# Weight chunks of the attention stage split by casting and accumulating DMAs from one pool of nine slots

## The chip, the core and the metric

The kernel runs on one core of one Trainium2 chip. The time is the device time of one execution in microseconds (us); the figure for a kernel is the median of its runs. Names used throughout: PE is TensorE, DVE is VectorE, ACT is ScalarE, POOL is GpSimd, SP is SyncE, whose queue issues most of the loads.

## What is computed

One layer of a streaming encoder on 256 tokens of width 2048, in float32. The cut below leaves out the shapes.

```python
h = rmsnorm(x, norm_in)
z, xbc, dt, q, k, v, gate_a, q_idx, k_idx, w_idx, gates = split(h @ w_in)
y_m = ssd_branch(z, xbc, dt, ...)       # causal convolution, chunked scan, silu gate, group norm
y_a = dsa_branch(q, k, v, gate_a, ...)  # index scores, top-64 keys of a query, softmax attention
g = sigmoid(gates + gate_bias)
merged = g[:, :D] * (y_m @ w_branch[:2048]) + g[:, D:] * (y_a @ w_branch[2048:])
x = rmsnorm(x + merged @ w_out, norm_final)
```

All the dense products stream their weights: `w_in`, `w_branch` and `w_out` lie in memory as 192 chunks `W[i]` of 128 x 2048 float32 (1 MiB each), in the order of use.

## The kernel before

**Split products.** A float32 product is made of three products of a shorter type (`F32R`): a weight chunk `raw` is rounded to `hi` by ACT (L121), and DVE forms the rest, `lo = raw - hi` (L122). The activations are kept as such a pair too (`xh`, `xl`). For every block PE adds `hi`·`xh`, `hi`·`xl` and `lo`·`xh` into one accumulator; so two of three products need `hi` alone, and every third one needs `lo`. With `hi` as stationary operand the result comes out transposed (`gemm_t`, `chunk_t`, L143 to L171: units "T" of two chunks, 48 products of 256 columns in each); with the activations stationary it comes out natural (`gemm_n`, `chunk_n`, L173 to L194: units "N" of four chunks, in each 12 products of 512 columns for either token block, accumulators `acc_n0` and `acc_n1`).

**The stream of weights.** `fetch` (L124) takes a `raw`, a `hi` and a `lo` tile, each from a pool of its own with three slots (L83 to L85), issues the load on SP (L134) and the split. `next_chunk` (L138) calls it until 1 + `AHEAD` = 3 chunks are ready, and hands out the oldest. `w_tiles` (L115) also serves the opening (L217 to L238), where x and the first two units' weights arrive in step in five pieces, and the small `w0` array (L246 to L249). `state["done"]` counts chunks consumed, `tick` (L105) then emits work that `after` (L101) put off.

**What sets the order.** The code is written as one program; a scheduler at build time lays the instructions out in one queue for each engine, by dependences and by when a slot of a pool comes free, and the engines run their queues in order. So where a chunk's split stands among the other work of ACT and DVE follows from the order in which the tiles of the pools are taken.

**The stages, in order**: the opening and the norm; four groups of the SSD mixer (`conv_silu`, `decay`, `natural_x`, `mix`, `transposed_y`, L373 to L470: DVE adds the skip term to PE's `py` at L435, makes the decays `E` at L393 and L396, ACT clips them at L399; the gate `sz` is evacuated at L479); the indexer and the top-k selection (`select`, L538: rounds of MAX8 and MATCH_REPLACE8, L550 and L551); branch A's gates and product; the `v` stage (four natural units, evacuated by ACT at L593); attention (eight rounds of three transposed units for keys, queries and gate, 48 chunks, with `attend`, `flip` and `weigh` of the heads between them); branch B's gates, and the second projection (four natural units: DVE multiplies by the gate, L690, adds to `merged`, L691, transposes it by 16 instructions, L680, ACT copies to `xh`, L682); the output product with the last norm.

Of the kernel before, what the change touches and what calls it, by code (L numbers as in the profile page):

```python
# [11 lines left out]
F32 = mybir.dt.float32  # L12
F32R = mybir.dt.float32r
# [17 lines left out]

# columns of the small-parameter array
PN, PCW, PCB, PGN, PDT, PAL = 0, 16, 112, 136, 152, 153
NPAR = 154
NWARM = 10  # products that bring the array to its full clock
PIECES = ((0, 2), (2, 4), (4, 8), (8, 12), (12, 16))  # row blocks of the first pieces
AHEAD = 2  # chunks of weights fetched ahead of the products


def unit_list():  # L40
    """The dense products in the order in which their weights stream in.

    ("T", source, first row, columns of the two blocks): transposed result, weights stationary.
    ("N", source, first row, first column): natural result, 512 columns, activations stationary.
    """
    us = []
    for g in range(4):
        us.append(("T", "in", 0, (B0 + 128 * g, C0 + 128 * g)))
        for a in range(2):
            c = XS0 + 512 * g + 256 * a  # L50
            us.append(("T", "in", 0, (c, c + 128)))
        us.append(("N", "in", 0, Z0 + 512 * g))
    for j in range(4):
        us.append(("T", "in", 0, (QI0 + 256 * j, QI0 + 256 * j + 128)))
    for j in range(4):
        us.append(("N", "in", 0, GM0 + 512 * j))
        us.append(("N", "br", 0, 512 * j))
    for j in range(4):
        us.append(("N", "in", 0, V0 + 512 * j))
    for j in range(8):  # L60
        for c in (K0, Q0, G0):
            us.append(("T", "in", 0, (c + 256 * j, c + 256 * j + 128)))
    for j in range(4):
        us.append(("N", "in", 0, GA0 + 512 * j))
    for j in range(4):
        us.append(("N", "br", D, 512 * j))
    for j in range(4):
        us.append(("N", "out", 0, 512 * j))
    return us


UNITS = unit_list()
NCHUNK = sum(2 if u[0] == "T" else 4 for u in UNITS)


@with_exitstack
def block_kernel(ctx, tc, W, w0, xT, xn, par, gbias, dsk, nf, out):
# [4 lines left out]
    acts = ctx.enter_context(tc.tile_pool(name="acts", bufs=1))  # L82
    wraw = ctx.enter_context(tc.tile_pool(name="wraw", bufs=3))  # L83
    whi = ctx.enter_context(tc.tile_pool(name="whi", bufs=3))
    wlo = ctx.enter_context(tc.tile_pool(name="wlo", bufs=3))  # L85
    dram = ctx.enter_context(tc.tile_pool(name="dram", bufs=1, space=DRAM))
# [8 lines left out]

    # ---------------------------------------------------------------- weights
    state = {"unit": 0, "chunk": 0, "done": 0}
# [3 lines left out]
    def after(n, fn):  # L101
        """Emit fn behind the products of the next n chunks, so that its operands are there in time."""
        pending.append((state["done"] + n, fn))
# [11 lines left out]
    def w_tiles():  # L115
        return (wraw.tile([P, 2048], F32, tag="raw", name="raw"),
                whi.tile([P, 2048], F32R, tag="hi", name="hi"),
                wlo.tile([P, 2048], F32R, tag="lo", name="lo"))

# [4 lines left out]
    def fetch(hi=None, lo=None):  # L124
        """Load the next chunk of weights and split it into two float32r parts."""
        i = state["chunk"]
        if i == NCHUNK:
            return
        state["chunk"] += 1
        if hi is None:  # L130
            raw, hi, lo = w_tiles()
        else:
            raw = wraw.tile([P, 2048], F32, tag="raw", name="raw")
        nc.sync.dma_start(raw, W[i])  # L134
        split(hi, lo, raw)
        ready.append((hi, lo))
# [24 lines left out]
    def gemm_t(ah, al):  # L161
        """acc[c, cb, t] = sum_k w[k, c] a[k, t] for the next transposed unit."""
        assert UNITS[state["unit"]][0] == "T"
        state["unit"] += 1
        acc = acc_tile("acc_t")
        for half in range(2):
            hi, lo = next_chunk()
            chunk_t(acc, hi, lo, half, range(8), ah, al)
            if half == 0:
                tick()  # L170
        return acc  # L171
# [11 lines left out]
    def gemm_n(ah, al):  # L183
        """acc[tb][t, c] for the next natural unit of 512 columns."""
        assert UNITS[state["unit"]][0] == "N"
# [9 lines left out]

    # ------------------------------------------------------- input, RMS norm
    part = const.tile([P, NPAR], F32, name="part")
# [14 lines left out]
    xTv = xT.rearrange("p (k t) -> p k t", t=T)  # L212
    # the array's clock rises under load: keep it busy until the first operands are there
    pw = aux_tile([P, P], "pw")
    for _ in range(NWARM):
        mm(pw, ones, ones, start=True, stop=True)
    # the first two units: x and their weights arrive in step, piece by piece  # L217
    acc_start = [acc_tile(f"acc_start{u}") for u in range(2)]
# [21 lines left out]
    for k0, k1 in PIECES:  # L240
# [3 lines left out]
                                axis=mybir.AxisListType.X, op=ALU.add)  # L244
    # k_idx (64), dt (32), w_idx (16)
    raw, hi, lo = w_tiles()  # L246
# [4 lines left out]
    for tb in range(2):  # L251
        for i, (k0, k1) in enumerate(PIECES):
            mm(prn[:, tb:tb + 1], xraw[:, k0, tb * P:tb * P + P], ones[:, 0:1],
               start=i == 0, stop=i == len(PIECES) - 1)
    # 1 / rms of every token: per partition, and along the free axis
    rn = const.tile([P, 2], F32, name="rn")
# [32 lines left out]

    # ------------------------------------------------ masks, dt and its sums  # L290
    tri = const.tile([P, 384], F32, name="tri")
# [31 lines left out]
    nc.vector.tensor_scalar(ab[H], dt[H], an[H], -1.0, ALU.mult, ALU.mult)  # L323
    # running sums within chunks of 64
    nc.vector.tensor_tensor_scan(al[H], rmask[H], ab[H], 0.0, ALU.mult, ALU.add)
# [37 lines left out]

    # -------------------------------------------------------------- SSD mixer

# [15 lines left out]
    def decay(g, acb, bc):  # L381
        """M[s, h, t] = exp(sum of dt a over s+1..t) (B_s . C_t) for t >= s, 0 before."""
        pcb = aux_tile([P, 384], "pcb")
# [34 lines left out]
    def mix(M, xdt, xD, sz):  # L418
        """Gated and normalised output of a group, natural layout."""
        ss = grp2.tile([P, 2], F32, tag="ss", name="ss")  # L420
# [66 lines left out]

    # ---------------------------------------------------------------- indexer
    mb = const.tile([P, 384], F32, name="mb")
# [3 lines left out]

    # keys for two heads at once: rows 0..63 give columns 0..255, rows 64..127 columns 256..511
    kbh = grp.tile([P, 2, T], F32R, tag="xdt", name="kbh")
# [8 lines left out]
    def index_scores(pair, qh, ql):  # L504
        """Adds the scores of heads 2 pair, 2 pair + 1 to sc."""
        cb = pair % 2
# [31 lines left out]
    def select():  # L538
        """mb: 0 for the keys that are chosen and finite, -BIG for the others."""
        # query chunk c sees the keys below 64 (c + 1)  # L540
        hidden = (slice(64, P), slice(P + 192, 384))
# [16 lines left out]

    # ------------------------------------------- branch A: gates and product
    def gates(acc, c0, out_ap):  # L560
        """sigmoid(projection + bias) of 512 columns, natural layout."""
        gb = tmp.tile([P, 512], F32, tag="gb", name="gb")
# [24 lines left out]

    # -------------------------------------------------------------- attention
    v = big.tile([P, 2, D], F32, tag="big", name="v")
# [7 lines left out]
    def attend(kT, qT, hh, le):  # L597
        """Attention weights of one head, natural layout, in blocks
        (queries 0, keys 0), (queries 1, keys 0), (queries 1, keys 1)."""
        pl = aux_tile([P, 384], "pl")  # L600
# [14 lines left out]
    def flip(les):  # L615
        """Keys on partitions: the same three blocks of both heads, each transposed."""
        t = tmp.tile([P, 2, 3, P], F32, tag="pT", name="pT", bufs=1)
# [42 lines left out]

    # ------------------------------------------- branch B: gates and product
    for j in range(4):
# [31 lines left out]

    # ---------------------------------------- output product, residual, norm
    x1 = big.tile([P, 2, D], F32, tag="big", name="x1")
# [11 lines left out]
    for j in range(4):  # L708
# [3 lines left out]
        if j < 3:  # L712
            if j == 2:
                # the last unit's four chunks stay on chip together
                hh = acts.tile([P, 2, 2048], F32R, tag="ya", name="hh")
                ll = acts.tile([P, 2, 2048], F32R, tag="yb", name="ll")
# [10 lines left out]
    for tb in range(2):  # L727
        r = rf[:, tb:tb + 1]
        # sum over the columns that are done, / D + EPS
        nc.vector.tensor_reduce(r, sf[:, tb, 0:3], axis=mybir.AxisListType.X, op=ALU.add)  # L730
# [73 lines left out]
```

## Time and profile before

| what | us |
|---|---|
| median of 3 runs | 1161.73 |
| lowest and highest run | 1160.87, 1162.21 |
| profiled execution: its span (the profile gives no other time of it) | 1159.6 |
| PE busy, of the span | 1146.9 (99%) |
| DVE busy | 753.6 (65%) |
| ACT busy | 544.1 (47%) |
| POOL busy | 13.4 (1%) |

The span runs from the first to the last instruction of one profiled execution. The rows of the section further down come from that execution: busy times of an engine in a stretch, mean durations of groups of instructions, and idle times with what ended them.

### The profile page before, as it was taken

The numbers are of one execution on the slowest core, as the hardware profiler recorded it, in microseconds if no ns is written. First come the engines' busy times: TensorE is split into PE (matmuls) and PEld (weight loads), VectorE is DVE, ScalarE is ACT, GpSimd is POOL, SyncE is SP. The second block draws the span as 40 slices with busy tenths as digits, with TensorE's granted clock in tenths as the row PEclk, the third lists the DMA queues.
The fourth block names the chain that finished last, engine by engine and source line by source line (L and its number), as shares of the span: only waits on it lengthen the run. The fifth ranks groups of instructions, "written<-read, shape, count | busy, mean of one in ns | idle before, by whom it ended". The sixth has DMA issues, their size and how long they took to land.

```text
span 1159.6 us, 16788 instructions
## 1 busy us (share of the span) xinstructions
PE 1146.9 (99%) x7174; PEld 1040.3 (90%) x7174; DVE 753.6 (65%) x931; ACT 544.1 (47%) x507; POOL 13.4 (1%) x29
## 2 busy tenths in 40 slices
PE   8999999999999999999999999999999999999997
PEld 8989898999988888888899999999999888888887
DVE  7899767685668445444447667766677455789662
ACT  7556765574444333334335434544444443343451
POOL 0001000000000000000000000000000000000000
PEclk9999999999999999999999999999999999999999
DMA  7755636354446556555554544545544566564652
GB/s 253 257 219 182 218 125 239 127 198 149 146 171 218 192 188 217 194 189 208 184 185 154 207 159 169 181 146 185 180 169 143 210 215 235 181 234 158 239 197 73
DMA packets 33979, 217.15 MB, mean 187 GB/s; under 512 B 3857, under 2 KB 4081, under 8 KB 9201
## 3 DMA queue, kind: packets, MB, share of 16 engines
q1 hardware_dynamic: 31248, 207.58, 51.0%
q10 hardware_dynamic: 2656, 8.50, 2.0%
q8 instruction: 56, 0.92, 0.3%
q14 instruction: 19, 0.15, 0.0%
HBM read 213.87 MB, written 2.13 MB: 186 GB/s over the span
## 4 chain that ended last, share of the span: by engine, by line
PE 93%; DVE 3%; DMA 2%; ACT 1%; issue 0%; POOLq 0%; DVEq 0%; SPq 0%; POOL 0%; ACTq 0%
PE acc_t L149 37%; PE acc_n L181 16%; PE acc_n L179 16%; PE acc_n L180 16%; DMA xraw<-xT 1%; DVE lo L122 1%; PE acc_last L181 1%; PE acc_last L180 1%; PE acc_last L179 1%; PE py L431 1%; PE py L433 1%; PE pl L602 1%; PE py L428 1%; PE po L629 1%; DMA raw<-W 1%; DVE c L376 1%
## 5 line engine op out<-in xcount | busy, mean ns | idle before, releaser
L122 DVE TENSOR_TENSOR lo<-raw,hi 128x2048 fp32r<-128x2048 f32 (+2 forms) x197 | 437.2, 2223 | 273.5 <-ACT hi L121 273.0
L121 ACT ACTIVATE hi<-raw 128x2048 fp32r<-128x2048 f32 (+2 forms) x197 | 366.3, 1861 | 468.2 <-PE acc_n L180 249.8
L149 PE MATMUL acc_t<-xh,hi 128*128 128x256 f32 x1216 | 320.9, 285 | 0.0
L149 PE MATMUL acc_t<-xl,hi 128*128 128x256 f32 x1216 | 317.9, 283 | 0.0
L149 PE MATMUL acc_t<-xh,lo 128*128 128x256 f32 x1216 | 244.9, 283 | 0.0
L181 PE MATMUL acc_n<-lo,xh 128*128 128x512 f32 x608 | 236.7, 389 | 0.3 <-DVE lo L122 0.3
L179 PE MATMUL acc_n<-hi,xh 128*128 128x512 f32 x608 | 237.0, 390 | 0.0
L180 PE MATMUL acc_n<-hi,xl 128*128 128x512 f32 x608 | 236.6, 389 | 0.0
L149 PEld LDWEIGHTS acc_t<-xl,hi 128*128 128x128 f32 x1216 | 233.4, 192 | 0.5
L149 PEld LDWEIGHTS acc_t<-xh,hi 128*128 128x128 f32 x1216 | 233.2, 192 | 0.5
L149 PEld LDWEIGHTS acc_t<-xh,lo 128*128 128x128 f32 x1216 | 189.6, 192 | 0.0
L181 PEld LDWEIGHTS acc_n<-lo,xh 128*128 128x128 f32 x608 | 114.1, 188 | 24.6 <-DVE lo L122 0.7
L180 PEld LDWEIGHTS acc_n<-hi,xl 128*128 128x128 f32 x608 | 114.2, 188 | 23.6
L179 PEld LDWEIGHTS acc_n<-hi,xh 128*128 128x128 f32 x608 | 114.2, 188 | 23.2
L180 PE MATMUL acc_n<-hi,yl 128*128 128x512 f32 x256 | 99.6, 389 | 0.0
L179 PE MATMUL acc_n<-hi,yh 128*128 128x512 f32 x256 | 99.6, 389 | 0.0
L181 PE MATMUL acc_n<-lo,yh 128*128 128x512 f32 x256 | 99.6, 389 | 0.0
L181 PEld LDWEIGHTS acc_n<-lo,yh 128*128 128x128 f32 x256 | 48.0, 188 | 10.3
L180 PEld LDWEIGHTS acc_n<-hi,yl 128*128 128x128 f32 x256 | 48.0, 188 | 10.0
L179 PEld LDWEIGHTS acc_n<-hi,yh 128*128 128x128 f32 x256 | 48.0, 188 | 9.8
L622 DVE STREAM_TRANSPOSE pT<-le 32x192 f32<-32x192 f32 x128 | 47.3, 370 | 1.9
L376 DVE SCALAR_TENSOR_TENSOR c<-u,part,c 128x255 f32<-128x255 f32 (+2 forms) x72 | 30.8, 479 | 2.0 <-ACT c L373 1.4
(201 smaller groups left out, 832.0 us busy)
## 6 DMA issues: line engine op xcount, KB each, us to landing
raw<-W SPq DMA_DIRECT2D x188, 1024.0 KB, 4.9
acb<-adr ACTq DMA_DIRECT2D x4, 1024.0 KB, 4.6
raw<-W SPq DMA_DIRECT2D x6, 512.0 KB, 8.6
gb<-gbias SPq DMA_DIRECT2D x8, 256.0 KB, 3.5
xr<-xn ACTq DMA_DIRECT2D x4, 512.0 KB, 5.3
xraw<-xT SPq DMA_DIRECT2D x3, 512.0 KB, 8.6
raw<-W SPq DMA_DIRECT2D x4, 256.0 KB, 5.7
nfb<-nf ACTq DMA_DIRECT2D x1, 1024.0 KB, 6.4
```

Source lines behind the costliest of these rows:

```text
L121: nc.scalar.activation(hi, raw, AF.Copy)
L122: nc.vector.tensor_sub(lo, raw, hi.bitcast(F32))
L149: mm(acc[:, cb, :], wv[:, k, cb], a[:, kk, :], start=first and kk == 0 and cb == 0, stop=last and kk == KB - 1, skip_group_check=True)
L179: mm(acc[:, c], ah[:, kk, ts], hv[:, k, c], start=kk == 0, stop=False)
L180: mm(acc[:, c], al[:, kk, ts], hv[:, k, c], start=False, stop=False)
L181: mm(acc[:, c], ah[:, kk, ts], lv[:, k, c], start=False, stop=kk == KB - 1)
L376: nc.vector.scalar_tensor_tensor(c[:, b, sh:], u[:, b, :T - sh], wv[3 - sh], c[:, b, sh:], ALU.mult, ALU.add)
L428: mm(py[:, hc], E[:, 0:P], xdt[:, 0, hc], start=h == 0, stop=h == 7, skip_group_check=True)
L431: mm(py[:, hc], E[:, P:T], xdt[:, 0, hc], start=h == 0, stop=False, skip_group_check=True)
L433: mm(py[:, hc], E[:, T:384], xdt[:, 1, hc], start=False, stop=h == 7, skip_group_check=True)
L602: mm(pl[:, P:384], qT[:, hh, P:T], kT[:, hh, :], start=False, stop=True, skip_group_check=True)
L622: nc.vector.transpose(t[sj, :, :, si], lv[si, :, :, sj])
```

## The change

- The three pools of three slots become one pool, `wpool`, of nine slots with one tag, so `raw`, `hi` and `lo` take slots from it in turn. `AHEAD` goes from 2 to 3.
- In the attention stage every second chunk from its fifth on, 22 of 48 (`BY_DMA`), takes two slots and not three, and is split in another way: POOL's queue issues a DMA from `W[i]` into `hi_d` that casts to F32R; ACT writes `-hi_d` into `lo_d`; POOL's queue issues a second DMA that adds `W[i]` onto `lo_d`. The `raw` tile, SP's load and DVE's subtraction of these chunks go.
- Comments are taken out; lines move by up to +9.

```diff
-AHEAD = 2  # chunks of weights fetched ahead of the products
+AHEAD = 3
@@
+NATT = NCHUNK - 4 * 12 - 48
+BY_DMA = frozenset(range(NATT + 4, NATT + 48, 2))
@@
-    wraw = ctx.enter_context(tc.tile_pool(name="wraw", bufs=3))
-    whi = ctx.enter_context(tc.tile_pool(name="whi", bufs=3))
-    wlo = ctx.enter_context(tc.tile_pool(name="wlo", bufs=3))
+    wpool = ctx.enter_context(tc.tile_pool(name="wpool", bufs=9))
@@
-        return (wraw.tile([P, 2048], F32, tag="raw", name="raw"),
-                whi.tile([P, 2048], F32R, tag="hi", name="hi"),
-                wlo.tile([P, 2048], F32R, tag="lo", name="lo"))
+        return (wpool.tile([P, 2048], F32, tag="w", name="raw"),
+                wpool.tile([P, 2048], F32R, tag="w", name="hi"),
+                wpool.tile([P, 2048], F32R, tag="w", name="lo"))
@@
         state["chunk"] += 1
+        if i in BY_DMA:
+
+            hi = wpool.tile([P, 2048], F32R, tag="w", name="hi_d")
+            lo = wpool.tile([P, 2048], F32R, tag="w", name="lo_d")
+            nc.gpsimd.dma_start(hi, W[i])
+            nc.scalar.activation(lo, hi.bitcast(F32), AF.Copy, scale=-1.0)
+            nc.gpsimd.dma_start(lo, W[i], accum_op=ALU.add)
+            ready.append((hi, lo))
+            return
         if hi is None:
             raw, hi, lo = w_tiles()
         else:
-            raw = wraw.tile([P, 2048], F32, tag="raw", name="raw")
+            raw = wpool.tile([P, 2048], F32, tag="w", name="raw")
```

How the build orders the queues, at three places. The number behind a name tells tiles of one name apart; `hi_`, `lo_` and `raw_` of one chunk have neighbouring numbers.

ACT, the boundary between the second and the third unit of the `v` stage. The evacuations are those of the accumulators `acc_n0_4450` and `acc_n1_4451`; that unit's last chunk is `hi_4483` before and `hi_4453` after. Before:

```order
L593 ACTIVATE v_4325<-acc_n1_4327,rn_412 128x512
L121 ACTIVATE hi_4483<-raw_4482 128x2048
L121 ACTIVATE hi_4513<-raw_4512 128x2048
L121 ACTIVATE hi_4543<-raw_4542 128x2048
L593 ACTIVATE v_4325<-acc_n0_4450,rn_412 128x512
```

After:

```order
L602 ACTIVATE v_4325<-acc_n1_4327,rn_406 128x512
L121 ACTIVATE hi_4389<-raw_4388 128x2048
L121 ACTIVATE hi_4419<-raw_4418 128x2048
L121 ACTIVATE hi_4453<-raw_4452 128x2048
L602 ACTIVATE v_4325<-acc_n0_4450,rn_406 128x512
L121 ACTIVATE hi_4483<-raw_4482 128x2048
L602 ACTIVATE v_4325<-acc_n1_4451,rn_406 128x512
```

Before, two chunks of the next unit (`hi_4513`, `hi_4543`) stand ahead of the evacuation of `acc_n0_4450`; after, none (the next unit begins with `hi_4483`).

DVE, the SSD mixer, where the output sums of the first group (`yt_2078`, behind PE's `py`) lie; the products on PE at that time are those of the unit `acc_n0_1881`, whose chunks are `hi_1761` (the first), `hi_1815`, `hi_1884` and `hi_1921` before, and `hi_1658` to `hi_1884` after. Before:

```order
L122 TENSOR_TENSOR lo_1922<-raw_1920,hi_1921 128x2048
L122 TENSOR_TENSOR lo_1952<-raw_1950,hi_1951 128x2048
L122 TENSOR_TENSOR lo_1982<-raw_1980,hi_1981 128x2048
L413 TENSOR_TENSOR xdt_1600<-px_2013,nat_604 128x2x256
L415 TENSOR_TENSOR xD_1601<-px_2013,dskb_602 128x2x256
L122 TENSOR_TENSOR lo_2025<-raw_2023,hi_2024 128x2048
L435 TENSOR_TENSOR yt_2078<-py_2079,xD_1601 128x512
L122 TENSOR_TENSOR lo_2117<-raw_2115,hi_2116 128x2048
L436 TENSOR_TENSOR yt_2078<-yt_2078,sz_2010 128x512
L435 TENSOR_TENSOR yt_2078<-py_2091,xD_1601 128x512
L393 TENSOR_TENSOR E_2329<-acb_2020,nat_604 128x4x256
```

After:

```order
L122 TENSOR_TENSOR lo_1816<-raw_1814,hi_1815 128x2048
L444 TENSOR_TENSOR yt_2078<-py_2079,xD_1601 128x512
L402 TENSOR_TENSOR E_2329<-acb_2020,nat_604 128x4x256
L405 TENSOR_TENSOR E_2329<-acb_2020,nat_604 128x4x128
L444 TENSOR_TENSOR yt_2078<-py_2091,xD_1601 128x512
L122 TENSOR_TENSOR lo_1885<-raw_1883,hi_1884 128x2048
L402 TENSOR_TENSOR E_2335<-acb_2020,nat_604 128x4x256
L405 TENSOR_TENSOR E_2335<-acb_2020,nat_604 128x4x128
L122 TENSOR_TENSOR lo_1922<-raw_1920,hi_1921 128x2048
L445 TENSOR_TENSOR yt_2078<-yt_2078,sz_2010 128x512 x2
L122 TENSOR_TENSOR lo_1952<-raw_1950,hi_1951 128x2048
```

Before, `lo_1922` and the two behind it, the last of that unit and the next ones, stand ahead of the sums; after, `lo_1885`, the last of that unit, and all later ones stand behind the sums and behind sums for `E`.

DVE, the second projection, behind its second unit, which is `acc_n0_8542` before and `acc_n0_8520` after; the unit's last chunk is `hi_8575` before and `hi_8523` after, `mt` and `merged` are the gated sum, `mT` its transposes. Before:

```order
L122 TENSOR_TENSOR lo_8576<-raw_8574,hi_8575 128x2048
L122 TENSOR_TENSOR lo_8606<-raw_8604,hi_8605 128x2048
L122 TENSOR_TENSOR lo_8636<-raw_8634,hi_8635 128x2048
L690 TENSOR_TENSOR mt_8664<-acc_n0_8542,ga_8000 128x512
L691 TENSOR_TENSOR merged_3431<-merged_3431,mt_8664 128x512
L690 TENSOR_TENSOR mt_8667<-acc_n1_8543,ga_8000 128x512
L691 TENSOR_TENSOR merged_3431<-merged_3431,mt_8667 128x512
L680 STREAM_TRANSPOSE mT_8670<-merged_3431 32x2x4x32 x16
L122 TENSOR_TENSOR lo_8693<-raw_8691,hi_8692 128x2048
L683 TENSOR_TENSOR xl_92<-mT_8670,xh_91 128x1024
L122 TENSOR_TENSOR lo_8723<-raw_8721,hi_8722 128x2048
```

After:

```order
L122 TENSOR_TENSOR lo_8524<-raw_8522,hi_8523 128x2048
L699 TENSOR_TENSOR mt_8642<-acc_n0_8520,ga_7978 128x512
L700 TENSOR_TENSOR merged_3431<-merged_3431,mt_8642 128x512
L122 TENSOR_TENSOR lo_8554<-raw_8552,hi_8553 128x2048
L699 TENSOR_TENSOR mt_8645<-acc_n1_8521,ga_7978 128x512
L700 TENSOR_TENSOR merged_3431<-merged_3431,mt_8645 128x512
L689 STREAM_TRANSPOSE mT_8648<-merged_3431 32x2x4x32 x10
L122 TENSOR_TENSOR lo_8584<-raw_8582,hi_8583 128x2048
L689 STREAM_TRANSPOSE mT_8648<-merged_3431 32x2x4x32 x6
L692 TENSOR_TENSOR xl_86<-mT_8648,xh_85 128x1024
L122 TENSOR_TENSOR lo_8614<-raw_8612,hi_8613 128x2048
L122 TENSOR_TENSOR lo_8671<-raw_8669,hi_8670 128x2048
```

Before, two later chunks (`lo_8606`, `lo_8636`) are split ahead of the multiplication, and the 16 transposes stand in one piece; after, the next chunk's `lo_8554` stands between the two halves of the gated sum, and `lo_8584` between the tenth and the eleventh transpose.

POOL's queue holds 44 DMAs more, `hi_d` and `lo_d` in turn.

## Rows read from the trace of the kernel before

**Rows 1.** The page, span and part 1: busy time and instructions of each engine.

```profile
span 1159.6 us, 16788 instructions
PE 1146.9 (99%) x7174; PEld 1040.3 (90%) x7174; DVE 753.6 (65%) x931; ACT 544.1 (47%) x507; POOL 13.4 (1%) x29
```

**Rows 2.** Waits of PE, whole span: us in total, times, longest us.

```profile
PE acc_start L149 <- ACT hi L121: 3.5, 4, 1.6
PE pw L216 <- POOL ones L200: 1.0, 1, 1.0
PE acc_n L181 <- DVE lo L122: 0.3, 1, 0.3
```

**Rows 3.** Windows: us, PE, PEld, DVE, ACT, POOL, PEclk, DMA, GB/s; last, `acc_t` alone.

```profile
500.00:560.00 60.00, 60.00 (x266) 49.67 (x266) 26.50 (x13) 23.77 (x16) 0.00 (x0) 1.00 0.56 193
600.00:880.00 280.00, 280.00 (x2296) 278.56 (x2295) 187.56 (x293) 125.33 (x129) 0.00 (x0) 1.00 0.48 170
...
600.00:880.00 280.00, 265.84 (x2184) 263.13 (x2183) 15.90 (x23) 1.00 0.48 170
```

**Rows 4.** Groups by form: count, busy us, mean ns of one, idle before.

```profile
L122 DVE TENSOR_TENSOR lo<-raw,hi 128x2048 fp32r<-128x2048 f32 x186 | 425.2, 2289 | 272.0 <-ACT hi L121 271.6
L121 ACT ACTIVATE hi<-raw 128x2048 fp32r<-128x2048 f32 x186 | 355.9, 1914 | 467.0 <-PE acc_n L180 249.8 <-PE acc_t L149 141.2 <-issue 65.8
...
L680 DVE STREAM_TRANSPOSE mT<-merged 32x256 f32<-32x256 f32 x64 | 27.9, 436 | 1.0
...
L691 DVE TENSOR_TENSOR merged<-merged,mt 128x512 f32<-128x512 f32 x8 | 5.5, 692 | 0.3
...
L690 DVE TENSOR_TENSOR mt<-acc_n,ga 128x512 f32<-128x512 f32 x8 | 5.5, 688 | 0.3
...
L593 ACT ACTIVATE v<-acc_n,rn 128x512 f32<-128x512 f32 x8 | 5.4, 678 | 4.1 <-PE acc_n L181 4.1
...
L682 ACT ACTIVATE xh<-mT 128x1024 fp32r<-128x1024 f32 x4 | 4.3, 1064 | 6.1 <-DVE mT L680 6.1
```

**Rows 5.** Waits of SP's queue, 10 to 26 us: us in total, times, longest.

```profile
SPq L227 <- DVE lo L122: 2.6, 1, 2.6
```

**Rows 6.** Timeline of ACT, 24 to 27 us: start, us, operation, idle before.

```profile
24.24 1.71 ACT L230 ACTIVATE xh<-xraw,part 128x256 fp32r<-128x256 f32 x4 [3.47 <-DMA xraw<-xT]
```

**Rows 7.** Groups by form, SSD mixer.

```profile
L399 ACT ACTIVATE E<-E 128x1536 f32<-128x1536 f32 x8 | 11.7, 1473 | 1.5 <-DVE E L396 1.5
...
L393 DVE TENSOR_TENSOR E<-acb,nat 128x1024 f32<-128x1024 f32 x8 | 9.7, 1217 | 0.0
...
L435 DVE TENSOR_TENSOR yt<-py,xD 128x512 f32<-128x512 f32 x8 | 5.5, 689 | 12.9 <-PE py L428 12.8
...
L396 DVE TENSOR_TENSOR E<-acb,nat 128x512 f32<-128x512 f32 x8 | 5.5, 684 | 0.0
...
L479 ACT ACTIVATE sz<-acc_n,rn 128x512 f32<-128x512 f32 x8 | 5.4, 676 | 3.0 <-PE acc_n L181 3.0
```

**Rows 8.** Groups by form, the top-k selection.

```profile
L550 DVE MAX8 m<-wk 128x8 f32<-128x256 f32 x8 | 3.3, 412 | 0.0
L551 DVE MATCH_REPLACE8 wk<-m,wk 128x256 f32<-128x256 f32 x8 | 3.2, 405 | 0.0
...
L550 DVE MAX8 m<-wk 128x8 f32<-128x128 f32 x8 | 2.2, 278 | 0.0
...
L551 DVE MATCH_REPLACE8 wk<-m,wk 128x128 f32<-128x128 f32 x8 | 2.2, 273 | 0.0
```

**Rows 9.** The page, part 3: DMA queue of SP; packets, MB, share.

```profile
q1 hardware_dynamic: 31248, 207.58, 51.0%
```

**Rows 10.** Tile `raw`: issue time in ns, then issue to landing in us.

```profile
L134 SPq DMA_DIRECT2D raw<-W x188: 327/328/328, 28.2 to 1121.8; - x188
...
DMA to landing us min/median/max: 4.2/4.9/10.6
```

## The prediction

> **What bounds the kernel now.** The page comes first: TensorE (PE) is busy for 1146.9 of the 1159.6 us of the span [rows 1]. The list of PE's waits then says how much of the rest can be had: 4.8 us, 3.5 of them at four places of the opening, and 0.3 once behind VectorE's (DVE's) `lo` [rows 2]. The windows tell how PE runs in the stages: in the `v` stage 266 products in 60 us, so 0.226 us for each of 512 columns; in the attention stage 2184 transposed products in 265.8 us of busy time, 0.122 us each. A chunk of 24 natural products takes 5.41 us, one of 48 transposed ones with its part of the heads' own products 280/(2184/48) = 6.15 us [rows 3]. DVE and ScalarE (ACT) are far from full. So the change can win almost nothing, since nothing in the attention stage waits for DVE; it loses wherever a chunk's two parts are no longer ready when PE arrives. The sum goes by that: for each place, what must run between the last thing PE gives and the next chunk's `lo`, less the products that PE still has in the meantime.
>
> Made against the profiled execution's span, 1159.6 us; the median of the runs, 1161.73, is 2.1 above it, and I add that at the end. Two runs of this kernel differ by 0.1%; 0.2% (2.3 us) is about what can be told from no change.
>
> **What goes.** In the attention stage 22 raw loads leave SP's queue and 22 `lo` subtractions leave DVE: 22 x 2.289 = 50 us of DVE [rows 4]. Worth nothing: PE never waited for them there. ACT keeps 22 operations of 2048 elements (a negation in place of the copy), as long as before [rows 4].
>
> At the start one thing is won. SP waits 2.6 us for a DVE `lo` before it may load into the next raw slot [rows 5], the last piece of x arrives late, and ACT idles 3.47 us for it [rows 6]. With nine slots the second pair of raw tiles takes fresh ones, the wait falls, and with it at most the 1.6 us that PE's longest opening wait lasts [rows 2]: I take -1.3.
>
> **What moves: splits outside attention.** This is the largest term. One tag allocates raw, `hi`, `lo` in program order, and the order places a chunk's split some two chunks (in the SSD mixer four) later among its neighbours on ACT and DVE than before. Nothing is longer; but these queues run in order, and a split now stands behind work that waits for PE's previous unit.
>
> The `v` stage, four boundaries. Before, two chunks of the next unit stand ahead of the evacuation; now none. From the last product of the first token block: evacuation 0.68, `hi` 1.91, `lo` 2.29 = 4.88 us [rows 4]. PE still has 12 products of the other block and 4 that need only `hi`: 16 x 0.226 = 3.61. Loss 1.3, and, an estimate, 0.3 for the hand-overs between engines; into attention only two short products need no `lo`, 0.7 more. 4 x 1.6 + 0.7 = **7**.
>
> The second projection, four units with the transposes of `merged`. Three gaps a unit: (a) multiply 0.69, add 0.69, `lo` 2.29 against the same 3.61, 0.4 with hand-overs; (b) multiply, add, ten transposes of 0.436, `lo`: 8.03 against one chunk of 5.41, 2.6; (c) six transposes 2.62, the copy to `xh` 1.06, `hi`, `lo`: 7.88 against 5.41, 2.5 [rows 4]. 4 x 5.5 = **22**.
>
> The SSD mixer and the indexer. In a group, (a) the sum behind `py` 0.69 [rows 7] and `lo` 2.29 = 2.98 against 4 products, 0.90: 2.1; (b) behind that `lo` the two sums for E 1.22 + 0.68, the ReLU on E 1.47, `hi`, `lo` = 7.57 against the other 20 products and two short ones, 4.76: 2.8 [rows 7]. The smaller gaps behind them (the other half's exponential, the convolution's rows ahead of a `lo`) I estimate at two thirds of these, 3.4, so 8.3 a group, 33 for four; the first two groups have dt's sums between the splits as well, for which I estimate 9 (none to 18). The indexer starts behind the gate `sz`, whose evacuation takes 0.68 [rows 7], as the `v` stage's boundary into attention does, and I put 3.4 more on the split behind the last group's norm: 2.3 + 3.4. Together **48**.
>
> The top-k selection: a round is 0.41 + 0.28 + 0.41 + 0.27 = 1.37 us [rows 8], eight rounds are 10.9 us of DVE, in which three splits now stand. Between `lo_3230` and `lo_3276` lie four and a half rounds, 6.2, and the `lo`: 8.45 against 5.41, 3.0; the gap ahead and the gates behind it give as much again and more: **8**. Gates and output units lose 0.2 to 1.2 in each, by my estimate some **5** in all, from the evacuations' 0.68 in front of a `lo`.
>
> Outside attention: 7 + 22 + 48 + 8 + 5 - 1.3 = 89.
>
> **What is added: 44 transfers from POOL.** No row of before shows a transfer issued by POOL, a cast or an accumulation. POOL's queue is `hi_d`, `lo_d` in turn: the cast lands, ACT negates (1.91), POOL issues the accumulation, and the next cast stands behind it. Every pair of chunks gives PE 2 x 6.15 = 12.3 us. The queue rows give a plain MiB 0.510 x 1159.6 / 198 = 2.99 us of all 16 engines; a raw load lands in 4.9 us at the median, 10.6 at most, and an issue takes 0.33 [rows 9, 10]. One round of POOL's chain is the accumulation's engine time, a cast's landing, the negation, two issues and some 0.2 of hand-overs.
>
> - Low: the accumulation costs a plain transfer: 2.99 + 4.9 + 1.91 + 0.66 + 0.2 = 10.7, under 12.3. Loss nothing but the entry into the stage, some 4.
> - High: it takes three plain ones and each cast lands at the slowest row's 10.6: 22.3, 10 over, 22 x 10 = 220.
> - Taken: it reads its source and its destination, so twice a plain one, 5.98: 13.7, 1.4 over. In each pair the engines then carry 2.99 + 2.99 + 5.98 = 12.0 of 12.3 us, so the raw loads between get in the way; I add 0.4. 22 x 1.8 = **40**, and 4 for the entry.
>
> The Trainium skill (Collectives: The Full Stack, The bandwidth ceiling) says that the DMA's add is costlier for its two source reads, not for the adding; no run here shows it, and it would make the accumulation 5.98, as taken. The Trainium skill (DMA: Bandwidth & Descriptors, Anatomy of one DMA, SWDGE path) fits a transfer from GpSimd as 2.0 us plus bytes at 436 GB/s, an estimate of 4.4 us for 1 MiB; the HWDGE row here has 4.9, and by the page's figure the chain would be 0.5 shorter and the sum 11 us less.
>
> **Sum:** 1159.6 + 89 + 44 = 1292.6, and 2.1 around the span: **1295 us**, 11% slower.
>
> **Rivals.**
> 1. *The accumulation is cheap*, the low case above: 1161.7 + 89 + 4 = 1255. For it: the DMA engines are at 48% in this stage [rows 3].
> 2. *Cast and accumulation are dear*: halfway to the high end, 6 over in each pair, 1161.7 + 89 + 132 + 4 = 1387, and up to 1475. For it: a loaded transfer lands in 10.6 instead of 4.9 [rows 10].
> 3. *POOL can't prepare a transfer while DVE works.* DVE is busy 187.6 of 280 us [rows 3]; two issues in a chain, each held 2.29 x 0.67 at most, add 3.1 to every pair: 1295 + 22 x 3.1 = 1363. The Trainium skill (SBUF — State Buffer, The "DVE blocks DMA" trap) describes this lock, for DVE's two-port modes; the `lo` here runs at 1.12 ns an element, no such speed, so it speaks little for it.
> 4. *Not slower.* The splits, though later in the queue, still finish under PE's remaining products, as the three chunks in flight are the same; only the opening's gain is left: 1161.7 - 1.3 = 1160.4. It is decided at the `v` boundary: evacuation, `hi` and `lo` would have to fit into 3.61 us, and the rows have 4.88. That the chip's scheduler reorders queues is not to be seen: ACT's rows stand in the trace in the program's order.
>
> **How the numbers follow.** The forecast has 0.52, rival 1 0.18, rival 2 0.20, rival 3 0.06, rival 4 0.04. Each slower case carries my uncertainty of the 89, some 15 either way. From 1245 to 1400 the range holds the forecast, rival 1 but for its lower fifth, rival 3 and over half of rival 2; outside are about 0.15. Faster 0.015, within 0.2% 0.025 (rival 4 alone), slower 0.96.
>
> **What would show it.** PE's waits should grow from 5 us to some 130, in the main behind DVE's `lo` and ACT's `hi`; at each `v` boundary two gaps of PE, about 0.5 and 1.4 us; in each unit of the second projection about 5.5. The opening's 3.47 us of ACT should shrink. In attention a POOL chain of about 14 us a pair, PE waiting for `lo_d`. The forecast is wrong if these stages outside attention stay without gaps, if the chain takes under 12 us, or if it takes over 17. The granted clock stays at 1.00 in every stage [rows 3] in my sum; PE's gaps of up to 3 us could change that, which no row of before shows.

## The result, and the profile after

The changed kernel takes **1303.13 us** (median of 4 runs, 1299.51 to 1305.36) against 1161.3: 1.1223 times as long, 95% interval 1.1203 to 1.1243. The profiled execution took 1302.55 us, its span is 1300.8, so 141.2 us more than the span of [rows 1].

The page of the changed kernel: the span, parts 1 and 2 (PE and its clock), the two queues that load weights, the landings.

```profile
span 1300.8 us, 16806 instructions
...
PE 1196.5 (92%) x7174; PEld 1060.8 (82%) x7174; DVE 705.8 (54%) x909; ACT 541.5 (42%) x509; POOL 43.1 (3%) x73
...
PE   9897989898998999999998998998998999888897
PEclk9998999899999999999999999999998999999999
...
q1 hardware_dynamic: 28080, 184.51, 38.8%
q0 software_dynamic: 6336, 46.14, 14.2%
...
raw<-W SPq DMA_DIRECT2D x166, 1024.0 KB, 5.6
hi_d<-W POOLq DMA_DIRECT2D x22, 1024.0 KB, 10.8
lo_d<-W POOLq DMA_DIRECT2D x22, 1024.0 KB, 8.1
```

The waits of PE in the changed kernel (us in total, times, longest), to be held against [rows 2].

```profile
PE acc_n L190 <- DVE lo L122: 37.5, 31, 2.4
PE acc_t L158 <- DMA lo_d<-W: 27.4, 17, 5.2
PE acc_t L158 <- DVE lo L122: 17.9, 13, 4.5
PE acc_n L188 <- ACT hi L121: 3.6, 7, 0.8
...
PE acc_start L158 <- ACT hi L121: 1.8, 3, 0.8
```

Two things are to be seen. The 55 us behind `lo` on DVE are the late splits, the 27 behind `lo_d` are the new transfers. And PE, with the same 7174 products, is busy for 1196.5 us and not 1146.9: some stretches run at half the clock, and the first products after a wait take longer (0.50 us in the rows below; the kernel before has 0.39 for these products). All of PE's waits together are 95.9 us, before 4.8: they make 91 of the 141 us, and PE's longer busy time the other 50.

The stages, from the start of the first product of a stage to that of the next one, read from the timelines of PE in the two traces:

| stage | before, us | after, us | more | forecast |
|---|---|---|---|---|
| opening | 33.9 | 32.7 | -1.2 | -1.3 |
| SSD mixer and indexer | 287.8 | 332.7 | 44.9 | 48 |
| branch A with the top-k selection | 176.2 | 188.7 | 12.5 | } 8 and 5 |
| branch B's gates | 88.4 | 91.1 | 2.7 | } |
| `v` | 87.0 | 93.8 | 6.8 | 7 |
| attention | 296.0 | 343.8 | 47.8 | 44 |
| second projection and output | 175.6 | 203.5 | 27.9 | 22 |

Two boundaries, PE's rows that have a wait, columns start, length, operation, idle before. First between the second and the third unit of the `v` stage, then in the second projection:

```profile
582.75 0.50 PE L188 MATMUL acc_n<-hi,xh 128*128 128x512 f32 x1 [0.32 <-ACT hi L121]
585.08 0.49 PE L190 MATMUL acc_n<-lo,xh 128*128 128x512 f32 x1 [1.13 <-DVE lo L122]
...
1112.70 0.50 PE L190 MATMUL acc_n<-lo,yh 128*128 128x512 f32 x1 [0.54 <-DVE lo L122]
1120.87 0.58 PE L190 MATMUL acc_n<-lo,yh 128*128 128x512 f32 x1 [2.43 <-DVE lo L122]
1128.82 0.50 PE L190 MATMUL acc_n<-lo,yh 128*128 128x512 f32 x1 [0.60 <-DVE lo L122]
```

The first two were forecast at 0.5 and 1.4. In the second projection 0.4, 2.6 and 2.5 were forecast; the third wait is 0.60, for a reason that the section on the clock gives. DVE's rows of the same stretch have the work in front of each `lo`, in the built order:

```profile
1109.03 0.69 DVE L699 TENSOR_TENSOR mt<-acc_n,ga 128x512 f32<-128x512 f32 x1 [9.18 <-PE acc_n L190]
1109.75 0.69 DVE L700 TENSOR_TENSOR merged<-merged,mt 128x512 f32<-128x512 f32 x1
1110.36 2.28 DVE L122 TENSOR_TENSOR lo<-raw,hi 128x2048 fp32r<-128x2048 f32 x1
1112.56 0.68 DVE L699 TENSOR_TENSOR mt<-acc_n,ga 128x512 f32<-128x512 f32 x1
1113.28 0.69 DVE L700 TENSOR_TENSOR merged<-merged,mt 128x512 f32<-128x512 f32 x1
1114.01 4.48 DVE L689 STREAM_TRANSPOSE mT<-merged 32x256 f32<-32x256 f32 x10
1118.52 2.29 DVE L122 TENSOR_TENSOR lo<-raw,hi 128x2048 fp32r<-128x2048 f32 x1
```

Each `lo` ends where PE goes on. POOL's rows for the two tiles in the changed kernel (ns, then first and last start in us; then issue to landing):

```profile
L134 POOL DMA_DIRECT2D hi_d<-W x22: 560/860/872, 659.1 to 959.4; - x22
DMA to landing us min/median/max: 5.6/10.8/13.5
...
L136 POOL DMA_DIRECT2D lo_d<-W x22: 861/866/897, 671.3 to 972.3; - x22
DMA to landing us min/median/max: 7.8/8.1/11.3
```

21 rounds from 659.1 to 959.4 are 14.3 us each, against PE's 296.0/24 = 12.33 for a pair of chunks. On the mean of these rounds the cast lands after 10.8, the negation starts 0.4 later and takes 1.9, the accumulation is issued 0.3 behind it and the next cast 0.9 behind that.

### The profile page after: what moved, and what is told of

Same layout as the page of the kernel before. It is cut to its first block, busy times and chain, and to the rows that moved or that the text cites. A ratio compares the mean times of both kernels' runs of the same rounds, so it can differ in the third digit from the quotient of the medians.

```text
span 1300.8 us, 16806 instructions
## 1 busy us (share of the span) xinstructions
PE 1196.5 (92%) x7174; PEld 1060.8 (82%) x7174; DVE 705.8 (54%) x909; ACT 541.5 (42%) x509; POOL 43.1 (3%) x73
## 4 chain that ended last, share of the span: by engine, by line
PE 45%; issue 24%; DVE 15%; ACT 7%; DMA 6%; POOL 3%; ACTq 0%; POOLq 0%; SPq 0%; DVEq 0%
PE acc_n L190 10%; PE acc_n L189 10%; PE acc_n L188 10%; PE acc_t L158 9%; DVE lo L122 8%; ACT hi L121 4%; DMA raw<-W 3%; DVE mT L689 2%; PE acc_start L158 1%; POOL hi_d L134 1%; POOL lo_d L136 1%; DVE c L385 1%; DMA lo_d<-W 1%; DMA hi_d<-W 1%; PE acc_last L190 1%
## 5 line engine op out<-in xcount | busy, mean ns | idle before, releaser
L158 PE MATMUL acc_t<-xh,hi 128*128 128x256 f32 x864 | 230.6, 288 | 1.4 <-ACT hi L121 1.3
L158 PE MATMUL acc_t<-xl,hi 128*128 128x256 f32 x864 | 228.5, 286 | 0.0
L158 PE MATMUL acc_t<-xh,lo 128*128 128x256 f32 x864 | 178.2, 288 | 17.9 <-DVE lo L122 17.9
L158 PEld LDWEIGHTS acc_t<-xh,hi 128*128 128x128 f32 x864 | 167.8, 194 | 3.1 <-ACT hi L121 2.6
L158 PEld LDWEIGHTS acc_t<-xl,hi 128*128 128x128 f32 x864 | 168.1, 195 | 0.5
L158 PEld LDWEIGHTS acc_t<-xh,lo 128*128 128x128 f32 x864 | 136.5, 195 | 20.7 <-DVE lo L122 20.6
L158 PE MATMUL acc_t<-xh,lo_d 128*128 128x256 f32 x352 | 78.0, 305 | 27.6 <-DMA lo_d<-W 27.4
L158 PE MATMUL acc_t<-xh,hi_d 128*128 128x256 f32 x352 | 97.5, 297 | 0.0
L158 PE MATMUL acc_t<-xl,hi_d 128*128 128x256 f32 x352 | 96.8, 295 | 0.0
L158 PEld LDWEIGHTS acc_t<-xh,lo_d 128*128 128x128 f32 x352 | 59.3, 207 | 31.6 <-DMA lo_d<-W 31.5
## 6 DMA issues: line engine op xcount, KB each, us to landing
hi_d<-W POOLq DMA_DIRECT2D x22, 1024.0 KB, 10.8
```

What stands on the lines that cost most here:

```text
L158: mm(acc[:, cb, :], wv[:, k, cb], a[:, kk, :], start=first and kk == 0 and cb == 0, stop=last and kk == KB - 1, skip_group_check=True)
```

## The experiments

Times are medians; ratios are to the kernel before, in runs on the same chip. Lengths of stages and rows are those of a run's profiled execution.

### The first four: one pool or the DMAs, adding or latency

**Run 1: the pool alone.**

```diff
-BY_DMA = frozenset(range(NATT + 4, NATT + 48, 2))
+BY_DMA = frozenset()
```

> The change without the DMA splits: one pool of nine slots and AHEAD = 3, every chunk split by ACT and DVE. Theory (two separate costs): the later splits outside attention cost what they cost in the changed kernel, 93 us over all stages but attention, and attention runs as before; 1161.3 + 93 = 1254 us (1245 to 1265), gaps of PE behind lo and hi at the same places, attention within 5 us of its 301 us. Rival 1 (the casting and accumulating DMAs load the DMA engines and the slots, and that disturbs the rest): 1161 to 1180. Rival 2 (one pool hurts attention just as much, the DMAs themselves cost little there): 1280 to 1300.

Measured: 1287.11 us, 1.1096 (1.1077 to 1.1116). That is in the range of rival 2; the theory, which left attention as before, falls. Outside attention the stages are those of the changed kernel to within 2.2 us (the second projection 105.6 us against 105.5, `v` 93.8 in both), but for branch B's gates, 96.0 against 91.1, into which the last round's late `lo` falls. And attention takes 324.7 us in place of 296.0. DVE's rows in one of its rounds show why:

```profile
697.84 4.96 DVE L631 STREAM_TRANSPOSE pT<-le 32x192 f32<-32x192 f32 x13
702.83 2.29 DVE L122 TENSOR_TENSOR lo<-raw,hi 128x2048 fp32r<-128x2048 f32 x1
705.16 1.15 DVE L631 STREAM_TRANSPOSE pT<-le 32x192 f32<-32x192 f32 x3
```

Thirteen transposes of the heads' weights stand ahead of a `lo`; PE waits 2.32 us for it, in seven of the rounds. PE's waits for `lo` in the attention stage, here and then in the changed kernel (us in total, times, longest):

```profile
PE acc_t L158 <- DVE lo L122: 17.8, 8, 2.3
...
PE acc_t L158 <- DVE lo L122: 1.6, 1, 1.6
```

So the pool alone makes 126 of the 142 us, and the DMAs only 16 on top: the two costs don't add, because the DMA chunks take 22 `lo` from DVE and put the chain of POOL in the place of those waits.

**Run 2: the DMAs alone,** in three pools.

```diff
+        if i in BY_DMA:
+            hi = whi.tile([P, 2048], F32R, tag="hi", name="hi_d")
+            lo = wlo.tile([P, 2048], F32R, tag="lo", name="lo_d")
...
```

> The DMA splits alone: the three pools of three slots and AHEAD = 2 of before, hi_d from the pool of hi, lo_d from that of lo. Theory: ACT and DVE have the order of before, so nothing is lost outside attention. In attention hi_d takes the slot of the chunk three before it, which comes free when PE ends that chunk; issue 0.9, landing 6 to 8, negation 1.9, issue 0.9 and the accumulation's 8.1 make 18 to 20 us, so two pairs of chunks take that and 12.3 us of products, 15.4 to 16.1 a pair against 12.5: 64 to 79 us more, 1225 to 1241 us. Rival 1 (POOL's queue alone sets the pace, 14.3 us a pair as in the changed kernel): 1161.3 + 44 = 1205. Rival 2 (with three pools the transfers hide): 1161.

Measured: 1244.28 us, 1.0729 (1.0699 to 1.0759), all of it in attention (379.3 us); elsewhere the stages have the lengths of before to within 1.9 us, and those 1.9 are the opening: 32.0 us, with the three pools, the same code in it as before and SP's wait of [rows 5]:

```profile
SPq L238 <- DVE lo L124: 2.6, 1, 2.6
```

Run 8, also with three pools, has 32.8. So an opening varies by that much from execution to execution. The rows of `hi_d` and of what it waited for (us, times):

```profile
L136 POOL DMA_DIRECT2D hi_d<-W x22: 562/562/755, 601.7 to 937.1; - x22
...
  PE acc_t L160: 402.5, 22
```

A round is (937.1 - 601.7)/21 = 16.0 us, as the slot theory had it (the time is 3 us above its range), and all 22 casts wait for PE to give a slot back. In the changed kernel that is so five times.

**Run 3: a plain second transfer.**

```diff
-            nc.gpsimd.dma_start(lo, W[i], accum_op=ALU.add)
+            nc.gpsimd.dma_start(lo, W[i])
```

> The changed kernel with the second DMA of a chunk made a plain casting one, which overwrites lo_d instead of adding to it (the part lo of these 22 chunks is left out of the computation: lo_d holds the rounded weights). Queues, slots and waits stay. Theory (the accumulation occupies the DMA engines for about two plain transfers, and the next cast stands behind it): the cast's landing falls from 10.8 us by 2.5 to about 8.3, lo_d's landing from 8.1 to about 5.5, POOL's chain from 14.3 us a pair to under PE's 12.5; attention 349 us becomes 305 to 315, and the time 1303 - 39 = 1264 us (1255 to 1272). Rival (issue, fixed latency of POOL's queue and the negation set the pace, not the adding): the chain stays over 14 us, 1298 to 1305.

Measured: 1259.93 us, 1.0855 (1.0839 to 1.0871).

```profile
q0 software_dynamic: 6336, 46.14, 10.6%
...
hi_d<-W POOLq DMA_DIRECT2D x22, 1024.0 KB, 6.3
lo_d<-W POOLq DMA_DIRECT2D x22, 1024.0 KB, 5.3
```

Attention is 299.5 us, 3.5 over that of before; PE waits for no `lo_d`. With the same pool, and all splits on ACT and DVE, run 1 has 324.7: without the adding, the DMA splits take nearly all of the late splits' cost in this stage away. The queue's share gives 0.106 x 1257.3/44 = 3.03 us of all engines for a casting transfer, and with it the changed kernel's 0.142 x 1300.8 = 184.7 leave (184.7 - 22 x 3.03)/22 = 5.4 for an accumulating one, 1.8 times as much. Both landings fall, the cast's by 4.5 us: it stands behind the accumulation of the chunk before.

**Run 4: the raw tile taken first.**

```diff
+        while len(raws) < 3 and state["raw"] < NCHUNK:
+            raws.append(wpool.tile([P, 2048], F32, tag="w", name="raw"))
+            nc.sync.dma_start(raws[-1], W[state["raw"]])
+            state["raw"] += 1
+        raw = raws.pop(0)
         if hi is None:
-            raw, hi, lo = w_tiles()
...
-        nc.sync.dma_start(raw, W[i])
+            hi = wpool.tile([P, 2048], F32R, tag="w", name="hi")
+            lo = wpool.tile([P, 2048], F32R, tag="w", name="lo")
```

> One pool of nine slots without DMA splits, as in the first run, but AHEAD = 2 and with each raw tile taken, and its load issued, two chunks ahead of the hi and lo tiles of its chunk. Theory (it is the turn in which the one pool gives out raw, hi and lo that ties a load to the slots of the chunk before it, and so puts the splits later in the queues): the splits stand where they stood before, no gaps outside attention; the opening keeps the changed kernel's gain of 1.2 us; 1160.1 us (1158.5 to 1161.5). Rival (one pool of nine costs by itself, by the slots that come free in another order, whatever the order of taking them): 1200 to 1254 us.

Measured: 1161.74 us, 1.0010 (1.0001 to 1.0019). One pool of nine costs next to nothing, 0.8 us, when raw tiles are taken early: the turn of taking was the cause, and neither the pool nor its size. `AHEAD`, also different here, is no likely part: when run 1's kernel is built with 2 in place of 3, no split of DVE or ACT comes to stand earlier (of DVE's 718 other instructions 678 have as many splits ahead of them, 40 one fewer); that kernel was not timed. What is left has its place, the first SSD group: with three pools a split stands ahead of `rbc` on DVE, here it stands behind it, while DVE idles 2.43 us. First a row of before, then two of this run, and PE's wait, which was 0.3 us in [rows 2]:

```profile
41.50 0.42 DVE L278 COPY rbc<-prb 128x256 f32<-128x256 f32 x1
...
39.21 0.42 DVE L291 COPY rbc<-prb 128x256 f32<-128x256 f32 x1 [2.43 <-PE prb L290]
40.58 2.29 DVE L123 TENSOR_TENSOR lo<-raw,hi 128x2048 fp32r<-128x2048 f32 x1
...
69.34 0.50 PE L194 MATMUL acc_n<-lo,xh 128*128 128x512 f32 x1 [1.85 <-DVE lo L123]
```

In this execution the SSD mixer is 3.2 us longer than before and the opening 1.2 shorter, 32.7 us as in the changed kernel. That this is the gain of the fresh slots, as forecast, the runs don't bear out: see run 2.

### The halved clock

In run 1's attention seven rounds have the same wait of 2.32 us. Three windows of it, from wait to wait, and a piece of the second behind its wait (us, PE, PEld, DVE, ACT, POOL busy, PEclk, DMA, GB/s):

```profile
702.58:742.33 39.75, 37.43 (x307) 37.02 (x305) 25.49 (x42) 16.63 (x18) 0.00 (x0) 1.00 0.45 159
742.33:783.56 41.23, 38.91 (x306) 38.50 (x305) 25.49 (x42) 16.63 (x18) 0.00 (x0) 0.96 0.43 154
...
865.81:905.55 39.74, 37.42 (x306) 37.01 (x305) 25.48 (x42) 16.63 (x18) 0.00 (x0) 1.00 0.46 160
...
745.20:748.40 3.20, 3.20 (x16) 3.20 (x16) 3.12 (x4) 0.00 (x0) 0.00 (x0) 0.50 0.75 256
```

The same work is 1.48 us longer where a stretch at a granted clock of 0.50 (1.2 of 2.4 GHz) follows the wait, as it does in five rounds of the seven. Two runs tried to fill the wait.

**Run 5: products in the wait, wrong place.**

```diff
+FILL = frozenset(range(104, 144, 6))
...
+        if not lo_last and state["popped"] - 1 in FILL:
+            for _ in range(18):
+                one(hv, ah, 0, 0, first=True)
```

> The first run's kernel (one pool, no DMA splits, 1287.1 us) with the first product of seven chunks of the attention stage issued 18 times more, at the seven places where its PE waits 2.32 us for a lo that stands behind transposes on DVE; the accumulator is started anew each time, so the result stays. In that run five of the seven gaps were followed by a stretch at a granted clock of 0.50, and those rounds took 41.1 to 41.2 us against 39.75 for the two without. Theory (the halved clock behind a gap is a cost of its own here, some 1.45 us, since no later wait absorbs it): with the gaps filled by 2.2 us of products PE's clock stays at 1.00 in the stage, every round takes 39.75 us, attention 330 becomes 322, the time 1287 - 8 = 1279 us (1277 to 1282). Rival (the halved clock costs nothing, the queues of DVE and ACT set the rounds): 1285 to 1290.

Measured: 1302.45 us, 1.1216 (1.1199 to 1.1233). A miss of mine: the waits lie in the chunks 103, 109 and so on, and the repeats came behind them. They were paid in full, 15 us, and say nothing of the clock.

**Run 9 (made after run 8, told here): the same in the right place,** `range(102, 144, 6)`.

> As the fifth run, with the 18 repeats one chunk earlier, at the first product of the unit in whose second chunk PE waits 2.32 us; the repeats start the accumulator anew, so the result stays. The fifth run put them behind that wait, into the next unit, and cost 7 x 18 x 0.12 = 15 us. Theory (what PE waits for hangs on the end of the unit before, so the repeats fill the wait, and the halved clock behind it, 1.45 us in five of the seven rounds, goes with it): waits in these seven places under 0.3 us, granted clock 1.00 in the rounds, 1287.1 - 5 x 1.45 = 1279.8 us (1278 to 1283). Rival (the halved clock costs nothing of its own): 1286 to 1290. Rival 2 (the repeats move the wait and are added again): 1302.

Measured: 1280.62 us, 1.1037 (1.1021 to 1.1054). Two of its rounds, from the repeats to the next ones:

```profile
693.03:732.77 39.74, 39.58 (x324) 39.17 (x323) 25.48 (x41) 16.64 (x18) 0.00 (x0) 1.00 0.45 159
732.77:772.52 39.75, 39.59 (x324) 39.18 (x323) 25.49 (x41) 16.63 (x18) 0.00 (x0) 1.00 0.45 160
```

126 more products made run 1's kernel 6.5 us faster. PE stays at 1.00 in these rounds, every one of them takes 39.75 us: the halved clock was a cost of its own there. It is not one everywhere. Three units of the second projection of the changed kernel:

```profile
1111.77:1139.60 27.83, 24.26 (x97) 18.92 (x96) 19.88 (x26) 8.39 (x5) 0.00 (x0) 0.94 0.42 151
1139.60:1167.43 27.83, 24.13 (x98) 18.86 (x96) 19.87 (x26) 8.38 (x5) 0.00 (x0) 0.94 0.42 151
1167.43:1195.25 27.82, 22.98 (x98) 17.72 (x96) 19.87 (x26) 8.38 (x5) 0.00 (x0) 1.00 0.43 151
```

With the halved clock or without it the unit takes 27.83 us. The slow products only use up the wait behind them, the third of each unit: 0.60 us after a slow stretch; without one that unit's third wait is 0.76 and a fourth of 1.11 follows it. DVE's chain sets the unit.

### Removing the chain's wait

**Run 6: raw tiles first, with the DMA splits.** Run 4 with `BY_DMA` and its branch of the change, DMA chunks left out of `raws`.

> The fourth run's kernel (one pool of nine, raw tiles taken first, 1161.7 us) with the DMA splits of the change. Theory (with splits in time everywhere else, attention is set by POOL's chain alone, cast, negation, accumulation, next cast, 14.3 us a pair of chunks as in the changed kernel): no gaps outside attention, attention 301 + 44 to 48, 1206 to 1212 us. Rival 1 (slots set it, as with three pools, 16 us a pair): 1240 to 1250. Rival 2 (the chain was slowed by the late splits of the chunks between): under 1190.

Measured: 1191.28 us, 1.0257 (1.0240 to 1.0274). Outside attention nothing more is lost than in run 4. Attention is 326.2 us, 30.2 over before; POOL's rounds are (884.7 - 599.3)/21 = 13.6 us by the casts' issues, shorter than in the changed kernel, though the landings are nearly the same (10.6 and 8.0; the cast's issue is 0.70). That is near rival 2: of the changed kernel's attention 17.6 us more come with the late splits, 3.5 of them as in run 3, some 15 by the longer rounds (21 x 0.7). Nearly half of these 15 us, 6.9, are the first two rounds (16.2 and 13.9 us in the changed kernel, 11.5 and 11.7 here): there the negation starts 4.3 and 2.6 us after its cast has landed, here 0.1. What makes the other rounds longer, by 0.4 us each, stays open.

**Run 7: the next cast ahead of the accumulation,** in run 6's kernel; `start_cast` takes the tile `hi_d` and issues its cast.

```diff
+            hi = cast.pop(i) if i in cast else start_cast(i)
...
             nc.scalar.activation(lo, hi.bitcast(F32), AF.Copy, scale=-1.0)
+            if i + 2 in BY_DMA:
+                cast[i + 2] = start_cast(i + 2)
             nc.gpsimd.dma_start(lo, W[i], accum_op=ALU.add)
```

> As the sixth run, but the cast of the next DMA chunk is put ahead of the accumulation in the program; in POOL's queue two of three casts then stand ahead of the accumulation of the chunk before, the third stays behind it for want of a slot. Theory (the wait of POOL's queue for the negation, with the next cast behind it, is what makes the chain longer than the transfers' own time; 8.4 us of engine time for cast and accumulation and 2.9 for a raw load fit under 12.5 a pair): two of three chains go under PE's pace, a third of the 46 us is left, 1165 to 1185 us. Rival (the engines' time sets it, whatever the order of issue): 1200 to 1212.

Measured: 1176.01 us, 1.0130 (1.0109 to 1.0151). Attention is 307.3 us; PE waits for `lo_d` 7 times:

```profile
PE acc_t L172 <- DMA lo_d<-W: 6.7, 7, 1.8
```

The same 44 transfers, the same bytes: what this order saves, half of run 6's loss and more, was not the engines' time. POOL's wait for the negation falls from 261.2 us to 124.8. The edit also takes the next `hi_d`'s slot earlier; the order of issue and that of the slots were not tried apart. The landings changed places, 8.6 for the cast and 11.0 for the accumulation.

**Run 8: every fourth chunk, three pools.** `range(NATT + 4, NATT + 48, 4)` in run 2's kernel.

> Three pools of three slots as in the second run (1244.3 us), with 11 chunks of the attention stage split by DMA in place of 22, every fourth. Theory (with three slots each such chunk has only from the end of the third chunk before it, two chunks or 12.3 us, for a latency of 17 to 18.4 us): each still costs 4.5 to 5.6 us of waiting and often a stretch of halved clock, 1.5: 11 x 4.5 to 7 = 50 to 77 us, 1211 to 1238 us. Rival (POOL's chain and the engines' load set the cost, which half as many chunks bring under PE's pace, 18.4 under 24.9): 1161 to 1172.

Measured: 1227.96 us, 1.0576 (1.0558 to 1.0595); (359.7 - 296.0)/11 = 5.8 us for each DMA chunk, against 83.3/22 = 3.8 in run 2. Half as many cost three quarters as much, which fits latency between a slot's return and its next use, and not load.

**Run 10: every fourth chunk, one pool, raw tiles first.**

> As the sixth run (one pool of nine, raw tiles first, 1191.3 us), with every fourth chunk of the attention stage split by DMA, 11 in place of 22. Theory (the cost is the chain's 13.8 us against the 12.3 of a pair, and the nine slots give the cast its slot early enough): against four chunks, 24.7 us, the chain hides, no wait for lo_d but at the first, 1161 to 1166 us. Rival (each such chunk costs some 1.4 us wherever it stands, by slots as with three pools or by load): 1174 to 1180; as dear as with three pools, 5.8 each: 1225.

Measured: 1169.64 us, 1.0084 (1.0067 to 1.0101), between theory and rival. Attention is 303.5 us, 7.5 over before; PE waits 5.5 us for `lo_d` in 7 places, and the clock stays at 1.00 there. The cast lands in 5.3 us, but the accumulation in 11.6 where every second chunk had 8.0. That the raw loads, which run ahead here, hold it up would explain this; it was not tried.

No run was faster than the kernel before.

## Why the prediction was right

Forecast 1295 us, measured 1303, inside the range and on the side given 0.96.

- **What bounds:** PE without gaps, and every late split a gap. Borne out in the main: PE waits for `lo` 55 us, before 0.3. But all waits were to be some 130 us and are 95.9; 49.6 us are longer busy time of PE, which the sum had at nothing. In the second projection slow products only take the place of a wait, so a sum by the queues holds there; in the rest of the changed kernel the two were not told apart.
- **The splits outside attention, 89 us:** 93.6 by the table. The `v` boundaries and the first two waits of the second projection came out to 0.3 us of the working. The third wait there was 0.6 to 1.9 and not 2.5, in part because slow products ran in it; with the three waits, the fourth and the longer first products a unit lost 27.83 - 21.77 = 6.06 us where 5.5 were forecast (96 x 0.2268 is the unit without waits). Branch A, branch B's gates and the output were put too low, by some 6, and the SSD mixer with the indexer too high, by 3 (in its working two thirds of 4.9 are 3.3 and not 3.4, half a microsecond in the 48).
- **The chain of POOL, 14.1 us a pair:** measured 14.3, and the accumulation at two plain transfers (5.98) is 5.4. But its parts were put together wrongly: I took the cast's landing as 4.9 and added the accumulation's engine time; in the rows both sit in the cast's landing, 10.8, and the issues are 0.56 to 0.90 and not 0.33. That the sum of a round came out is in this part luck. Run 3 shows that the adding is what makes it long. The Trainium skill (Collectives: The Full Stack, The bandwidth ceiling) puts the price of such an add down to its second source read; the runs agree in size, 5.4 us against 3.0, and can't show the cause.
- **The step that failed:** "Worth nothing: PE never waited for them there", of the 22 `lo` that leave DVE in the attention stage; and the splits that move late were counted outside attention alone. With the late order attention loses 29 us when all its splits stay on DVE (run 1). The sum was saved, by luck, by the chain taking the place of those waits. So "89 for the move, 44 for the transfers" has the right sizes of the stages, and the wrong shares of the causes: 126 for the move alone, 16 for the transfers on top of it, 83 for the transfers alone with the old slots.
- **"The granted clock stays at 1.00"** was wrong: 0.974 over the run. It cost nothing in the second projection, where a queue sets the pace; where none does, it was 1.48 us for each stretch (run 1, and run 9 gave 6.5 us back for five of them).
- **Rivals:** 1, a cheap accumulation, falls by run 3; 2, a dearer chain, by its 14.3 us. 3, POOL held by DVE: the accumulations' issues last 861 to 897 ns and the casts' 560 to 872, where the rival needs 1.5 us more for each, and the parts of a round add up to 14.3 with no room for 3.1 more. The Trainium skill (SBUF — State Buffer, The "DVE blocks DMA" trap) ties such a lock to DVE's two-port modes; no run here shows one. 4, not slower, falls by the two waits at the `v` boundary.
- **The opening, -1.3:** the number came out, -1.2, and the reason falls. With the three pools and SP's wait of 2.6 us run 2's opening is as short (32.0; the one-pool runs have 31.8 to 33.3); ACT's 3.47 us of [rows 6] were a late piece of x in that one execution.

## What to carry over

One pool with one tag hands out slots in program order; a load that shares it with the tiles made from it is bound to their slots, and moves that work behind other work in queues that run in order. Take the loaded tile early (run 4), or give it a pool of its own, as the kernel before does, and compare the built order of the queues before the times. In a chain of transfers on one queue, count what stands behind a waiting issue, and the time from a slot's return to its next use; issue the next transfer ahead of the one that waits.

## What was not expected of the hardware

- An accumulating DMA of 1 MiB took 5.4 us of all 16 engines, a casting one 3.0, and its issue on POOL 0.86 us against 0.54 (run 3).
- Behind waits of PE of 2.32 us a stretch at half the clock followed in five of seven equal places and not in the other two (run 1); 126 extra products in those waits made the kernel 6.5 us faster.
- Two costs of 126 and 83 us, each measured alone, gave 142 together.
